# A hybrid S5 / RG-LRU decoder layer: the feed-forward block's first operands placed over other memory, and the S5 stages set later

## The chip, the cores and the metric

The kernel runs on one core of one Trainium2 chip. The metric is the device time of one execution in microseconds (us); every number here is in us unless it says otherwise. The engines are named as in the profile: PE (TensorE, matrix multiply), PEld (its weight loads), DVE (VectorE), ACT (ScalarE), POOL (GpSimd), SP (SyncE, which issues every DMA here; SPq is its queue).

## The reference

One layer on x of 2048 tokens by 1024 channels, float32:

```python
h = rms_norm(x, norm1_g)
proj = h @ w_in                      # 1024 -> 1536: u | xr | yr, 512 each
s5_out  = s5_mixer(u, ...)           # 32 groups of 16 channels, 64 complex states each,
                                     # a linear scan over time, then GELU and a sigmoid GLU
lru_out = rglru_mixer(xr, yr, ...)   # causal conv(4), sigmoid gates, gated linear scan, times GELU(yr)
mix = concat(rms_norm(s5_out), rms_norm(lru_out))
x = x + mix @ w_out
h2 = rms_norm(x, norm2_g)
x = x + (silu(h2 @ w_gate) * (h2 @ w_up)) @ w_down     # 1024 -> 2816 -> 1024
return rms_norm(x, final_g)
```

## The kernel before

**Precision and tiles.** Every large product is made of three matmuls on a high and a low part: high weight by high operand, high by low, low by high. ACT casts the high part (`whi`, `xh`), DVE or POOL subtracts it from the source to get the low part (`wlo`, `xl`). One matmul is 128x128 by 128x512. The 2048 tokens are four blocks of 512.

**Stages.** (1) Input projection, block by block (`in_tb`, 12 units of 24 matmuls each), with the recurrence's convolution, gates, decay and scan. Beside it `s5_build`, `s5_table`, `s5_w`, `s5_cp`, `s5_k`, `s5_i` and `s5_d_build` make S5's matrices and store them in the DRAM tensor `md`. (2) S5 in two halves (g = 0: blocks 0 and 1; g = 1: blocks 2 and 3), eight steps each: `s5_in` (matmuls and products), `s5_scan` (scans on DVE, products on DVE and POOL), `s5_out` (line 864 multiplies by `s_s`). The input goes through the DRAM tensor `ub`, the output through `zb`; `zload` (line 897) reads `zb` back. (3) `glu_tb` makes S5's GLU of a block and the mix: `norm_split` writes the normed operands of w_out, for even blocks in eight pieces of pool Q (`aH`, `aL`), for odd ones in `actH` and `actL` of pool A. (4) `out_pair(0)` for blocks 0 and 1 and `out_pair(2)` for 2 and 3: eight units m for each block; the evacuation (line 992) adds x, line 994 stores the sum in `x1d`, and `SumSq.finish` stores the row of scales in `r2d` (line 272). (5) The feed-forward block (FFN): gate and up products as Strassen-like products 1 to 7 on 2x2 blocks, in the order `PRODS = (1, 6, 2, 7, 5, 4, 3)`, for p = 0 (blocks 0 and 1), then p = 1; each of 11 steps s has a gate unit and an up unit of 84 matmuls (line 1209). (6) w_down (line 1349) and the final norm.

**FFN's first operands.** `combos` loads two rows of x1d and the scales into `hx` (line 1078, 1080), DVE norms them (line 1084), and DVE and POOL make the sums of the blocks in tiles `ht` (lines 1092 to 1095). For p = 0 `x_first` does so for k = 0 to 3 and splits the results at once into `xh` and `xl` (`split_x2`, lines 1049 and 1050), except products 5 and 3 (`LATE`), which go to the DRAM tensor `xcd` (line 1116), since their tiles lie in pool D2, over pool A; `x_load` reads these back (line 1139) and splits them. For p = 1 `x_ahead` stores all seven products early in FFN, and `x_load` reads them when p = 0 is done.

**What sets the order.** Every piece of work is put on a list with a time, `at(t, fn)`, in plan units. The list is run in the order of time, and a scheduler that models the engines then orders each engine's instructions; so the times are priorities. `ts0 = 130` is the time of the first S5 half, `tb_(t) = 18 + 2.2 * t` that of the pieces of the build. Each engine and SP's queue then run strictly in their order.

**Memory.** Pools are opened as a stack from the left (P, Q, L) and from the right (A, W, then S). `open_d1` closes L, Q and S and opens D1 over them, with the tiles of FFN; a tile of D1 waits for the readers of what lay there.

Of the kernel before, what the change touches and what calls it, by code (L numbers as in the profile page):

```python
# [9 lines left out]
F32 = mybir.dt.float32  # L10
# [7 lines left out]
SEQ, DM, TB = 2048, 1024, 512  # L18
# [41 lines left out]
class Plan:  # L60
# [3 lines left out]
    def at(self, t, fn):  # L64
        self.ev.append((t, len(self.ev), fn))
# [10 lines left out]
PRODS = (1, 6, 2, 7, 5, 4, 3)  # L76
# [3 lines left out]
def build(tc, nc, I, O, ctx):  # L80
# [10 lines left out]
    sA, sQ = ExitStack(), ExitStack()  # L91
    A = sA.enter_context(tc.tile_pool(name="A", bufs=1, side="right", reuse_waits="tile"))
    Q = sQ.enter_context(tc.tile_pool(name="Q", bufs=1, reuse_waits="tile"))
# [1 line left out]
    actL = A.tile([128, 8, TB], F32, name="actL")  # L95


    def piece(i, j, name):
        return Q.tile([128, 2, TB], F32, tag=f"pc{i}{j}", name=f"{name}{j}")

    pieces = {}

    def area(i):
        def chunk(k):
            if (i, k // 2) not in pieces:
                pieces[i, k // 2] = piece(i, k // 2, "aH" if i == 0 else "aL")
            return pieces[i, k // 2][:, k % 2, :]
        return chunk
# [100 lines left out]
    def mm3(ps, u, ks, H, L, first, last):  # L209
        n = len(ks)  # L210
        for i, (kw, kx) in enumerate(ks):
            part = u.parts[kw // 4]
            for j, (w, x) in enumerate((("hi", H), ("hi", L), ("lo", H))):
                PE.matmul(ps, lhsT=part[w][:, kw % 4, :], rhs=r_(x(kx)),  # L214
                          start=first and i == 0 and j == 0, stop=last and i == n - 1 and j == 2)
# [73 lines left out]
    def load_chunk(src, b, k, pool=A, tag="xc", bufs=4):  # L289
        t = pool.tile([128, TB], F32, tag=tag, name=tag, bufs=bufs)  # L290
        SP.dma_start(t, src[k * 128:(k + 1) * 128, b * TB:(b + 1) * TB])
        return t
# [261 lines left out]
        TS(out=cL, in0=s, scalar1=8.0, scalar2=None, op0=ALU.mult)  # L554
        TS(out=cLh, in0=s, scalar1=-4.0, scalar2=None, op0=ALU.mult)

    ts0 = 130

    def s5_start():
        with tc.issue_after(last["rs"]):  # L560
            s5_build()

    def tb_(t):
        return 18 + 2.2 * t

    at(18, s5_start)
    at(12.0, lru_decay)
    for half in range(2):
        for lev in range(7):
            at(tb_(1.0 + 5 * half + 0.7 * lev), lambda half=half, lev=lev: s5_table(half, lev))  # L570
# [27 lines left out]

    at(1.0, lru_start)
    xrp = [piece(0, i, "xr") for i in range(2)]  # L600
    v_xr = [t.rearrange("p a b -> p (a b)")[:, 0:TB + 4] for t in xrp]
    v_xh = [piece(1, 2, "xh"), piece(0, 2, "xh")]
    v_y, v_us = piece(0, 3, "y"), piece(1, 1, "us")
    v_hh, v_hl = piece(1, 0, "hh"), piece(1, 3, "hl")
# [281 lines left out]
    def pair(b):  # L886
        return (areaH, areaL) if b % 2 == 0 else (chunks_of(actH), chunks_of(actL))
# [76 lines left out]
    def out_bank():  # L964
        n = last["bank"] = last.get("bank", -1) + 1
        return acc() if n % 4 < 2 else aux("gt", 2)

    def out_pair(b0, t0):

        sums = {b: SumSq(8, ("sum", "sumh")[b % 2], dv=b >= NB - 2) for b in (b0, b0 + 1)}
        blocks = (b0, b0 + 1)
        order = [(m, b) for b in blocks for m in (0, 1)]
        order += [(m, b) for m in range(2, 6 if b0 == 0 else 8) for b in blocks]
        if b0 == 0:
            order += [(m, b) for b in blocks for m in (6, 7)]
        units = {}
        for n, (m, b) in enumerate(order):  # L980
            cur = C[b]
            t = t0 + n * 8 * PT + (32 * PT if b0 == 0 and n >= 12 else 0)
            if m not in units:
                units[m] = Unit(t, I["w_out"][m], 8, GP if m % 3 == 1 else DV)

            def prod(m=m, b=b, cur=cur, u=units[m]):
                cur["o", m] = out_bank()
                mm3(cur["o", m], u, [(k, k) for k in range(8)], *pair(b), True, True)

            def post(m=m, b=b, cur=cur):  # L990
                xc = cur.pop(("x", m))
                DV.tensor_tensor(out=xc, in0=cur.pop(("o", m)), in1=xc, op=ALU.add)
                sums[b].add(xc)
                SP.dma_start(x1d[b // 2][128 * m:128 * m + 128, TB * (b % 2):TB * (b % 2) + TB], xc)

            at(t - 5, lambda m=m, b=b, cur=cur: cur.__setitem__(("x", m), load_chunk(xT, b, m)))
            at(t, prod)
            at(t + 8 * PT + 0.5, post)
            if m == 7:
                at(t + 8 * PT + 4.0, lambda b=b: sums[b].finish(r2d[b // 2][TB * (b % 2):TB * (b % 2) + TB]))  # L1000
# [20 lines left out]
    D = {}  # L1021

    def open_d1():
        sL.close()
        sQ.close()
        sS.close()
        D["1"] = sD1.enter_context(tc.tile_pool(name="D1", bufs=1, reuse_waits="tile"))

# [4 lines left out]
    def d1(tag, bufs=1, dt=F32, w=TB):  # L1033
        return D["1"].tile([128, w], dt, tag=tag, name=tag, bufs=bufs)
# [3 lines left out]

    def xtile(c, j, k, dt=R, name=None):

        tag = f"x{c}{j}{k}"
        return D["2" if j in LATE else "1"].tile([128, TB], dt, tag=tag, name=name or tag, bufs=1)

    BANK = {1: "A", 2: "A", 6: "B", 7: "B", 4: "B", 5: "C", 3: "C"}
    FIRST = (1, 6, 5)
    LATE = (5, 3)

    def split_w(raw, eng, hi, lo):
        AC.copy(hi, raw)  # L1049
        eng.tensor_tensor(out=lo, in0=raw, in1=hi.bitcast(F32), op=ALU.subtract)  # L1050
        return hi, lo
# [19 lines left out]
    def combos(p, k, t):  # L1071

        cur = {}

        def load():
            for i in range(2):
                cur[i] = d1("hx", 3, w=2 * TB)
                SP.dma_start(cur[i], x1d[p][128 * (k + 4 * i):128 * (k + 4 * i) + 128])
            rs = cur["rs"] = d1("hx", 3, w=2 * TB)
            SP.dma_start(rs, r2d[p].unsqueeze(0).to_broadcast([128, 2 * TB]))  # L1080

        def norm():
            for i in range(2):
                DV.scalar_tensor_tensor(out=cur[i], in0=cur[i], scalar=pc("g2", k + 4 * i), in1=cur["rs"],
                                        op0=ALU.mult, op1=ALU.mult)

        def sums():
            a, c = cur[0], cur[1]
            b11, b12, b21, b22 = a[:, 0:TB], a[:, TB:], c[:, 0:TB], c[:, TB:]
            T = {j: d1("ht", 4) for j in (5, 7, 6, 4)}  # L1090
            a, c = (GP.tensor_tensor, (GP if p else DV).tensor_tensor)
            a(out=T[5], in0=b12, in1=b11, op=ALU.subtract)
            c(out=T[7], in0=b22, in1=b12, op=ALU.subtract)
            c(out=T[6], in0=T[7], in1=b11, op=ALU.add)
            a(out=T[4], in0=b21, in1=T[6], op=ALU.subtract)
            T.update({1: b11, 2: b21, 3: b22})
            cur["T"] = T

        at(t - 5.0, load)
        at(t, norm)  # L1100
        at(t + 0.5, sums)
        return cur

    def split_x2(p, j, k, src, eng):
        H, L = (xtile(c, j, k) for c in "hl")
        X[p, j, k] = split_w(src, eng, H, L)

    def x_first(p, t):
        for k in range(4):
            tk = t + 6.0 * k  # L1110
            cur = combos(p, k, tk)

            def fin(k=k, cur=cur):
                for i, j in enumerate(PRODS):
                    if j in LATE:
                        SP.dma_start(xcd[p, k, :, j - 1, :], cur["T"][j])
                    else:
                        split_x2(p, j, k, cur["T"][j], GP if i % 3 == 2 else DV)

            at(tk + 2.0, fin)  # L1120

    def x_ahead(p, ts):
        for k in range(4):
            cur = combos(p, k, ts[k])

            def fin(k=k, cur=cur):
                for j in PRODS:
                    SP.dma_start(xcd[p, k, :, j - 1, :], cur["T"][j])

            at(ts[k] + 4.0, fin)  # L1130

    def x_load(p, times):
        for i, j in enumerate(times):
            for k in range(4):
                cur = {}

                def load(j=j, k=k, cur=cur):
                    cur["t"] = d1("ht", 4)
                    SP.dma_start(cur["t"], xcd[p, k, :, j - 1, :])

                t = times[j] + (k - 4) * 0.65
                at(t - 5.0, load)
                at(t - 1.5, lambda i=i, j=j, k=k, cur=cur: split_x2(p, j, k, cur["t"], GP if (i + k) % 2 else DV))
# [121 lines left out]
    def down(t0):  # L1265
# [93 lines left out]
        def row_tile(p, q, i):  # L1359
            r = RR[p, q, i] = xtile("hl"[p], {2: 7, 0: 5, 1: 4, 3: 3}[q], i, F32, f"r{q}")  # L1360
            return r
# [86 lines left out]
    gt = {}  # L1448
# [6 lines left out]
    tD = T  # L1455

    at(tC - 128 * PT + 4.0, open_d1)
    at(tC + 1.0, open_d2)
    x_first(0, tC - 128 * PT + 12.0)
    x_load(0, {j: gt[0, 0, 0, j] for j in LATE})  # L1460
    x_ahead(1, [gt[0, 3 + 2 * k, 0, 1] for k in range(4)])
    x_load(1, {j: gt[1, 0, 0, j] for j in PRODS})
    for p in range(2):
# [5 lines left out]
    pl.run()  # L1469
    sD2.close()  # L1470
    sD1.close()


def layout(x, norm1_g, w_in, s5_lambda_re, s5_lambda_im, s5_log_step, s5_b_re, s5_b_im, s5_c_re, s5_c_im,
# [78 lines left out]
```

## Time and profile before

| what | us |
|---|---|
| time, median of 3 runs | 2196.97 (2190.81 to 2200.07) |
| the profiled execution's own time | 2196.63 |
| its span, first to last instruction | 2194.9 |
| PE busy | 1964.2 (89% of the span) |
| DVE busy | 1207.0 (55%) |
| POOL busy | 1016.9 (46%) |
| ACT busy | 802.2 (37%) |
| last matmul of w_out for blocks 2 and 3 | 768 |
| first FFN matmul | 771 |

Busy times are summed over instructions; matmuls overlap in PE's pipeline, so a busy PE is not a PE at its peak, and the granted clock (PEclk) says how fast it ran. "DVE x <- PE y" in the views of waits reads: idle time of DVE ahead of x that ended when PE finished y.

### The profile page before, as it was taken

Reading aid. Unit: us, or ns where it says so; the run is one execution under the profiler, and the core shown is the slowest. Engines: PE = TensorE matmul, PEld = TensorE weight load, DVE = VectorE, ACT = ScalarE, POOL = GpSimd, SP = SyncE. Lnnn points to the kernel's source line nnn. Section 1 sums busy time; section 2 is a strip of 40 time slices with the busy share of each in tenths; the row PEclk is TensorE's granted clock in tenths of the full one; section 3 lists DMA queues with packets and bytes.
Section 4 is the critical chain, followed back from the end, with each engine's and each line's share of the span. In section 5 each row is a group of like instructions: output and inputs, shape, how many; then the busy total and the mean of one; then the engine's idle time right before and its main releaser. Section 6 shows DMA issues by size and latency. Waiting matters only on the chain.

```text
span 2194.9 us, 25988 instructions
## 1 busy us (share of the span) xinstructions
PE 1964.2 (89%) x8600; PEld 1564.3 (71%) x8600; DVE 1207.0 (55%) x1927; ACT 802.2 (37%) x1308; POOL 1016.9 (46%) x836
## 2 busy tenths in 40 slices
PE   5749898987989938799999999999999999999996
PEld 4637676765767816577777777777777788888785
DVE  5997676388447377444444474444444535654644
ACT  4535553463253123232232252232232343333331
POOL 1576255389533067654554561322312436644442
PEclk8969998988999958899999999999999999999998
DMA  8646997976543458644444484444444568854733
GB/s 290 215 151 202 297 253 260 223 193 189 148 122 117 158 187 282 220 163 145 144 158 144 156 260 131 137 142 133 144 131 130 171 221 317 298 171 143 238 101 101
DMA packets 259814, 405.21 MB, mean 185 GB/s; under 512 B 60224, under 2 KB 82016, under 8 KB 259680
## 3 DMA queue, kind: packets, MB, share of 16 engines
q1 hardware_dynamic: 259680, 403.56, 58.2%
q8 instruction: 67, 1.10, 0.2%
q14 instruction: 67, 0.55, 0.1%
HBM read 280.51 MB, written 122.96 MB: 184 GB/s over the span
## 4 chain that ended last, share of the span: by engine, by line
PE 67%; DVE 13%; DMA 7%; POOL 5%; ACT 3%; issue 3%; SPq 1%; POOLq 0%; DVEq 0%; ACTq 0%
PE acc L1209 9%; PE gt L1209 9%; PE y L1209 9%; PE acc L214 8%; PE v L1209 5%; PE nm L1209 5%; PE acc L1349 4%; PE y L1349 4%; PE gt L1349 4%; PE gt L214 3%; PE nm L1349 2%; PE v L1349 2%; POOL s_s L854 1%; DMA ht<-xcd 1%; DMA wraw<-w_in 1%
## 5 line engine op out<-in xcount | busy, mean ns | idle before, releaser
L1222 POOL TENSOR_TENSOR t<-t 128x512 f32<-128x512 f32 x66 | 100.8, 1528 | 348.6 <-DVE t L1248 219.4
L1049 ACT CAST whi<-ws 128x512 fp32r<-128x512 f32 x176 | 109.3, 621 | 347.3 <-PE y L1209 89.5
L214 PE MATMUL acc<-actH,whi 128*128 128x512 f32 x424 | 177.8, 421 | 43.1 <-DVE gy L712 14.8
L214 PE MATMUL acc<-actL,whi 128*128 128x512 f32 x424 | 177.3, 418 | 17.8 <-DVE actL L296 16.5
L214 PE MATMUL acc<-actH,wlo 128*128 128x512 f32 x424 | 174.9, 413 | 2.3 <-DMA wlo<-wlc 2.0
L1050 DVE TENSOR_TENSOR wlo<-ht,whi 128x512 fp32r<-128x512 f32 x112 | 106.8, 955 | 125.9 <-ACT whi L1049 123.8
L1049 ACT CAST whi<-ht 128x512 fp32r<-128x512 f32 x154 | 95.0, 618 | 167.8 <-PE nm L1349 72.4
L1209 PE MATMUL y<-xh,whi 128*128 128x512 f32 x308 | 125.5, 407 | 30.6 <-ACT xh L1049 16.3
L1050 DVE TENSOR_TENSOR wlo<-ws,whi 128x512 fp32r<-128x512 f32 x176 | 133.2, 757 | 33.0 <-ACT whi L1049 32.8
L1050 DVE TENSOR_TENSOR wlo<-wraw,whi 128x512 fp32r<-128x512 f32 x88 | 71.3, 810 | 143.4 <-ACT whi L1049 143.3
L1209 PE MATMUL acc<-xh,wlo 128*128 128x512 f32 x308 | 123.8, 402 | 10.3 <-DVE wlo L1050 10.3
L214 PEld LDWEIGHTS acc<-actH,whi 128*128 128x128 f32 x424 | 85.0, 201 | 67.3 <-issue 24.1
L1050 POOL TENSOR_TENSOR wlo<-ht,whi 128x512 fp32r<-128x512 f32 x42 | 58.3, 1389 | 159.2 <-ACT whi L1049 159.1
L1209 PE MATMUL acc<-xh,whi 128*128 128x512 f32 x308 | 124.1, 403 | 8.2 <-ACT xh L1049 6.6
L1209 PE MATMUL y<-xl,whi 128*128 128x512 f32 x308 | 124.1, 403 | 7.1 <-DVE xl L1050 7.1
L1209 PE MATMUL acc<-xl,whi 128*128 128x512 f32 x308 | 123.7, 402 | 7.0 <-DVE xl L1050 7.0
L1209 PE MATMUL y<-xh,wlo 128*128 128x512 f32 x308 | 123.7, 402 | 2.6 <-DVE wlo L1050 2.6
L1209 PE MATMUL gt<-xh,whi 128*128 128x512 f32 x308 | 121.4, 394 | 0.0
L1209 PE MATMUL gt<-xh,wlo 128*128 128x512 f32 x308 | 121.3, 394 | 0.0
L1209 PE MATMUL gt<-xl,whi 128*128 128x512 f32 x308 | 121.3, 394 | 0.0
L214 PEld LDWEIGHTS acc<-actL,whi 128*128 128x128 f32 x424 | 85.3, 201 | 40.6 <-DVE actL L296 22.7
L1049 ACT CAST whi<-wraw 128x512 fp32r<-128x512 f32 x88 | 54.6, 621 | 159.6 <-PE y L1209 53.0
(459 smaller groups left out, 5432.4 us busy)
## 6 DMA issues: line engine op xcount, KB each, us to landing
td<-t SPq DMA_DIRECT2D x154, 256.0 KB, 2.1
ht<-td SPq DMA_DIRECT2D x154, 256.0 KB, 3.2
wraw<-w_down SPq DMA_DIRECT2D x99, 256.0 KB, 4.8
wraw<-w_in SPq DMA_DIRECT2D x96, 256.0 KB, 4.8
scd<-ws SPq DMA_DIRECT2D x88, 256.0 KB, 2.1
ws<-scd SPq DMA_DIRECT2D x88, 256.0 KB, 2.7
wlo<-wlc SPq DMA_DIRECT2D x72, 256.0 KB, 5.3
xc<-xT SPq DMA_DIRECT2D x56, 256.0 KB, 4.7
```

Source lines behind the costliest of these rows:

```text
L214: PE.matmul(ps, lhsT=part[w][:, kw % 4, :], rhs=r_(x(kx)), start=first and i == 0 and j == 0, stop=last and i == n - 1 and j == 2)
L854: GP.tensor_tensor(out=sv[64 * ri:64 * ri + 64, gl, :, 1:], in0=a[p], in1=c[p], op=op)
L1049: AC.copy(hi, raw)
L1050: eng.tensor_tensor(out=lo, in0=raw, in1=hi.bitcast(F32), op=ALU.subtract)
L1209: PE.matmul(ps, lhsT=a[:, k, :], rhs=x, start=j in FIRST and k == 0 and i == 0, stop=k == 3 and i == 2, skip_group_check=True)
L1222: (DV if q == 0 else GP).tensor_tensor(out=g, in0=c, in1=g, op=ALU.mult)
L1349: PE.matmul(BK[p][i], lhsT=a[:, i, :], rhs=x, start=j in FIRST and s == 0 and v == 0, stop=s == NSL - 1 and v == 2, skip_group_check=True)
```

## The change

Four things are edited. The tiles of products 7 and 4 (`INQ`) for FFN's operands take the eight pieces of pool Q, two k in each, and Q stays open to the end, so that D1 lies over L and S only. `x_first` splits products 1, 6 and 2 (`AHEAD`) at once and sends 7, 5, 4 and 3 through `xcd`, where before only 5 and 3 went. `out_pair(2)` takes units 6 and 7 block by block, as `out_pair(0)` did. And the build's stretch grows from 2.2 to 2.9 plan units a step, with the first S5 half at 150 instead of 130.

```diff
@@ -95,8 +95,8 @@
     actL = A.tile([128, 8, TB], F32, name="actL")
 
 
-    def piece(i, j, name):
-        return Q.tile([128, 2, TB], F32, tag=f"pc{i}{j}", name=f"{name}{j}")
+    def piece(i, j, name, dt=F32):
+        return Q.tile([128, 2, TB], dt, tag=f"pc{i}{j}", name=f"{name}{j}")
 
     pieces = {}
 
@@ -554,14 +554,14 @@
         TS(out=cL, in0=s, scalar1=8.0, scalar2=None, op0=ALU.mult)
         TS(out=cLh, in0=s, scalar1=-4.0, scalar2=None, op0=ALU.mult)
 
-    ts0 = 130
+    ts0 = 150
 
     def s5_start():
         with tc.issue_after(last["rs"]):
             s5_build()
 
     def tb_(t):
-        return 18 + 2.2 * t
+        return 18 + 2.9 * t
 
     at(18, s5_start)
     at(12.0, lru_decay)
@@ -973,9 +973,8 @@
         sums = {b: SumSq(8, ("sum", "sumh")[b % 2], dv=b >= NB - 2) for b in (b0, b0 + 1)}
         blocks = (b0, b0 + 1)
         order = [(m, b) for b in blocks for m in (0, 1)]
-        order += [(m, b) for m in range(2, 6 if b0 == 0 else 8) for b in blocks]
-        if b0 == 0:
-            order += [(m, b) for b in blocks for m in (6, 7)]
+        order += [(m, b) for m in range(2, 6) for b in blocks]
+        order += [(m, b) for b in blocks for m in (6, 7)]
         units = {}
         for n, (m, b) in enumerate(order):
             cur = C[b]
@@ -1022,7 +1021,6 @@
 
     def open_d1():
         sL.close()
-        sQ.close()
         sS.close()
         D["1"] = sD1.enter_context(tc.tile_pool(name="D1", bufs=1, reuse_waits="tile"))
 
@@ -1038,12 +1036,20 @@
 
     def xtile(c, j, k, dt=R, name=None):
 
+        if j in INQ:
+
+            key = c, j, k // 2
+            if k % 2 == 0:
+                D[key] = piece("hl".index(c), 2 * INQ.index(j) + k // 2, name or f"x{c}{j}", dt)
+            return D[key][:, k % 2, :]
         tag = f"x{c}{j}{k}"
         return D["2" if j in LATE else "1"].tile([128, TB], dt, tag=tag, name=name or tag, bufs=1)
 
     BANK = {1: "A", 2: "A", 6: "B", 7: "B", 4: "B", 5: "C", 3: "C"}
     FIRST = (1, 6, 5)
     LATE = (5, 3)
+    INQ = (7, 4)
+    AHEAD = (1, 6, 2)
 
     def split_w(raw, eng, hi, lo):
         AC.copy(hi, raw)
@@ -1112,7 +1118,7 @@
 
             def fin(k=k, cur=cur):
                 for i, j in enumerate(PRODS):
-                    if j in LATE:
+                    if j not in AHEAD:
                         SP.dma_start(xcd[p, k, :, j - 1, :], cur["T"][j])
                     else:
                         split_x2(p, j, k, cur["T"][j], GP if i % 3 == 2 else DV)
@@ -1457,7 +1463,7 @@
     at(tC - 128 * PT + 4.0, open_d1)
     at(tC + 1.0, open_d2)
     x_first(0, tC - 128 * PT + 12.0)
-    x_load(0, {j: gt[0, 0, 0, j] for j in LATE})
+    x_load(0, {j: gt[0, 0, 0, j] for j in PRODS if j not in AHEAD})
     x_ahead(1, [gt[0, 3 + 2 * k, 0, 1] for k in range(4)])
     x_load(1, {j: gt[1, 0, 0, j] for j in PRODS})
     for p in range(2):
@@ -1469,6 +1475,7 @@
     pl.run()
     sD2.close()
     sD1.close()
+    sQ.close()
 
 
 def layout(x, norm1_g, w_in, s5_lambda_re, s5_lambda_im, s5_log_step, s5_b_re, s5_b_im, s5_c_re, s5_c_im,
```

In what the scheduler makes of it, line numbers past 1040 are 6 higher than before, those from 976 to 1020 one lower. DVE, at the end of w_out for blocks 2 and 3 (xc: an evacuation; sum, sumh: sums of squares; hx: the norm of a round; ht: its sums; xl: a low part). Before:

```order
L992 TENSOR_TENSOR xc<-gt,xc 128x512
L255 TENSOR_TENSOR sum<-sum,sq 128x512
L992 TENSOR_TENSOR xc<-gt,xc 128x512
L1084 SCALAR_TENSOR_TENSOR hx<-hx,par 128x1024 x2
L227 TENSOR_SCALAR nm<-nm 128x4
L255 TENSOR_TENSOR sumh<-sumh,sq 128x512
L1050 TENSOR_TENSOR xl_5838<-hx,xh_5837 128x512
L1093 TENSOR_TENSOR ht<-hx 128x512
```

and now:

```order
L991 TENSOR_TENSOR xc<-acc,xc 128x512
L1090 SCALAR_TENSOR_TENSOR hx<-hx,par 128x1024 x2
L255 TENSOR_TENSOR sum<-sum,sq 128x512
L1056 TENSOR_TENSOR wlo<-wraw,whi 128x512
L1056 TENSOR_TENSOR xl_6076<-hx,xh_6075 128x512
L1099 TENSOR_TENSOR ht<-hx 128x512
L991 TENSOR_TENSOR xc<-gt,xc 128x512
L1056 TENSOR_TENSOR wlo<-ws,whi 128x512
L1100 TENSOR_TENSOR ht<-ht,hx 128x512
```

Before, this is the norm of k = 0, behind the last evacuation. Now it is that of k = 3, with two evacuations still to come; the norms of k = 0, 1 and 2 stand 8, 6 and 3 evacuations ahead of that one.

SP's queue, the loads of products from xcd (ht<-xcd) where FFN begins. Before:

```order
L1078 DMA hx<-x1d_85 128x1024 x2
L1139 DMA ht<-xcd 128x512 x2
L1080 DMA hx<-r2d_87 128x1024
L1139 DMA ht<-xcd 128x512
L1167 DMA scd<-ws 128x512
L1139 DMA ht<-xcd 128x512 x3
```

and now:

```order
L993 DMA x1d_85<-xc 128x512
L1084 DMA hx<-x1d_85 128x1024
L1145 DMA ht<-xcd 128x512
L1173 DMA scd<-ws 128x512
L1145 DMA ht<-xcd 128x512
L1163 DMA wraw<-w_gate 128x512
L1122 DMA xcd<-ht 128x512
L1145 DMA ht<-xcd 128x512
L993 DMA x1d_85<-xc 128x512
L1173 DMA scd<-ws 128x512
L1145 DMA ht<-xcd 128x512
```

The loads, 8 before and 16 now, begin behind the last but one store of x1d (unit 7 of block 3 is the last), where before they came after all of w_out and of the four rounds.

POOL, at the last low part of the mix of blocks 0 and 1 (actL; s_k, s_s, s_wr and s_wi are S5's second half). Before:

```order
L854 TENSOR_TENSOR s_s<-s_tb,s_wi 64x2x128 x2
L854 TENSOR_TENSOR s_s<-s_ta,s_wr 64x2x128 x2
L303 TENSOR_TENSOR actL<-nf,actH 128x512
L812 TENSOR_TENSOR s_wr<-s_wr,s_ta 128x256
L813 TENSOR_TENSOR s_wi<-s_wi,s_tb 128x256
L854 TENSOR_TENSOR s_s<-s_tb,s_wi 64x2x128 x2
```

and now:

```order
L303 TENSOR_TENSOR actL<-nf,actH 128x512
L812 TENSOR_TENSOR s_wr<-s_wr,s_ta 128x256
L813 TENSOR_TENSOR s_wi<-s_wi,s_tb 128x256
L832 COPY s_s<-cy 64x2 x4
L833 TENSOR_TENSOR s_k<-cy,mi 128x2
```

Before, one S5 step ended behind it, now three do. In the two orders the first 372 instructions of DVE are the same, and on PE all from FFN's 104th matmul to the end.

## The prediction

> **What bounds the kernel now.** I read the page's slices first, then busy time by stage, then what TensorE (PE) waits for in the worst stage. Section 2 of the page, 40 slices of 55 us, tenths busy, and the granted clock:
>
> ```profile
> PE   5749898987989938799999999999999999999996
> PEclk8969998988999958899999999999999999999998
> ```
>
> From slice 16 on PE is full at full clock; the bad places are the first four slices, slices 9 and 10, and slices 14 and 15 (760 to 880 us), where the feed-forward (FFN) begins. There I cut the time where the output projection ends (768.0), where FFN's first full runs begin (836.9), and where the loss ends (908.1), counting FFN's matmuls alone (columns: stretch, length, PE busy (count), weight loads, clock, DMA share, GB/s):
>
> ```profile
> 768.00:836.90 68.90, 21.57 (x43) 11.00 (x43) 0.58 0.63 209
> 836.90:908.10 71.20, 55.12 (x210) 43.09 (x211) 0.86 0.82 276
> 908.10:988.60 80.50, 78.48 (x337) 62.86 (x336) 1.00 0.48 161
> ```
>
> The third row is the steady state: 80.5 / 337 = 0.2389 us a matmul. So the first stretch is worth 43 x 0.2389 = 10.3 us and loses 58.6; the second is worth 50.2 and loses 21.0. Together 79.6 us, the largest loss in the trace outside the first 250 us. What PE waits for from 768 to 910:
>
> ```profile
> PE y L1209 <- ACT xh L1049: 16.3, 4, 5.1
> PE acc L1209 <- DVE wlo L1050: 10.3, 1, 10.3
> PE y L1209 <- DVE xl L1050: 7.1, 4, 3.3
> PE acc L1209 <- DVE xl L1050: 7.0, 3, 5.3
> ```
>
> xh and xl are FFN's first operands, high and low part. They are made in four rounds (k = 0 to 3), which follow one another on VectorE (DVE) at the pace of their first instruction, the norm of line 1084; the queue says when they could have begun and what the first load waited for (last row: total, times, longest):
>
> ```profile
> 792.20 2.48 DVE L1084 SCALAR_TENSOR_TENSOR hx<-hx,par 128x1024 f32<-128x1024 f32 x2
> 805.17 2.48 DVE L1084 SCALAR_TENSOR_TENSOR hx<-hx,par 128x1024 f32<-128x1024 f32 x2 [4.05 <-DMA hx<-r2d]
> 818.50 2.48 DVE L1084 SCALAR_TENSOR_TENSOR hx<-hx,par 128x1024 f32<-128x1024 f32 x2 [4.42 <-DMA hx<-r2d]
> 709.53 0.27 SPq L272 DMA_DIRECT2D r2d<-row  x1
> SPq L1078 <- PE gt L214: 2.7, 2, 2.4
> 690.87 0.74 DVE L301 SCALAR_TENSOR_TENSOR nf<-wg,par,rs 128x512 f32<-128x512 f32 x1
> 746.02 11.06 PE acc L214 x48
> ```
>
> A round takes 13.2 us. Its inputs, x1d and r2d of blocks 0 and 1, are complete once the store of 709.53 has landed, 58.5 us before 768. The first load waited for PE's read of block 2's operands: FFN's memory lies over them. The last two rows serve below: the last norm of block 3's mix on DVE, and two units (48 matmuls) of the output projection, 5.53 us each.
>
> **The change, part by part.**
>
> *First operands out of the pieces' memory.* The D1 pool now lies over the L and S pools alone, which the last mix of block 3 leaves at 691 us, and in the new order of instructions the four norms stand among the evacuations of the second output projection (w_out) instead of behind them. Is there time? Rounds at 13.2 us from 709.5 plus the median landing of hx (row below) give norms at 715, 728, 742 and 755; the order puts the fourth behind the evacuation of the third unit from the end, 10 us before 768. Its splits take a round's 8.1 us of DVE (worked out below). So the operands of products 1, 6 and 2 are ready when PE wants them. Is there room? The stage before, all engines (PE, weight loads, DVE, ACT, POOL, clock, DMA), and the moved groups as they ran from 768 to 836.9 (busy us, mean ns | idle before):
>
> ```profile
> hx<-r2d SPq DMA_DIRECT2D x8, 512.0 KB, 5.8
> 712.00:768.00 56.00, 56.00 (x245) 45.55 (x244) 17.50 (x25) 11.30 (x18) 4.03 (x4) 1.00 0.49 155
> L1084 DVE SCALAR_TENSOR_TENSOR hx<-hx,par 128x1024 f32<-128x1024 f32 x10 | 12.5, 1294 | 10.7 <-DMA hx<-r2d 10.7
> L1050 DVE TENSOR_TENSOR xl<-hx,xh 128x512 fp32r<-128x512 f32 x4 | 7.0, 1740 | 0.0
> L1093 DVE TENSOR_TENSOR ht<-hx 128x512 f32<-128x512 f32 x4 | 7.1, 1763 | 0.0
> L1094 DVE TENSOR_TENSOR ht<-ht,hx 128x512 f32<-128x512 f32 x4 | 3.7, 928 | 0.3
> L1050 DVE TENSOR_TENSOR xl<-ht,xh 128x512 fp32r<-128x512 f32 x9 | 10.1, 1123 | 2.3 <-ACT xh L1049 2.2
> L1092 POOL TENSOR_TENSOR ht<-hx 128x512 f32<-128x512 f32 x4 | 8.8, 2210 | 15.1 <-DVE hx L1084 15.1
> L1166 POOL TENSOR_TENSOR ws<-wraw 128x512 f32<-128x512 f32 x2 | 3.0, 1516 | 1.2 <-DVE nv L235 1.2
> L1095 POOL TENSOR_TENSOR ht<-hx,ht 128x512 f32<-128x512 f32 x4 | 6.5, 1623 | 4.5 <-DVE ht L1094 4.5
> ```
>
> DVE gets four rounds of 2 x 1.294 + 1.740 + 1.763 + 0.928 + 1.123 = 8.1 us, 32.6 in all, beside its 17.5 of 56: it fits. POOL gets some 22 us and eight weight sums of 1.5 beside its 4. What waits behind a norm that waits for its hx is an evacuation, and PE has four banks, so it can run three units, 16.6 us, before it misses one. I let the end of w_out slip by 1 us (0 to 13).
>
> *Products 7, 5, 4 and 3 through memory.* Before, only 5 and 3 of these went out to xcd and back. Now all four do: 16 tiles, 8 stores and 8 loads more, through four ht buffers, each load behind the split of the one four earlier. The nearest row is the same loading at the change from p = 0 to 1 (first and last row of 24 loads):
>
> ```profile
> 1267.71 2.02 SPq L1139 DMA_DIRECT2D ht<-xcd  x3
> 1303.17 1.57 SPq L1139 DMA_DIRECT2D ht<-xcd  x2
> ht<-xcd SPq DMA_DIRECT2D x36, 256.0 KB, 3.5
> ```
>
> 24 tiles in 37 us is 1.54 us a tile, 24.7 for 16. The loads stand in SP's queue around the last two stores of x1d, so the first goes out 1 us before PE ends w_out, and the last tile is split 24.7 + 3.5 + 2 us later, at +29. Ahead of it PE has the 72 other matmuls of the unit and up to 30 that the order draws forward from the up unit, about 24 us. So 5 us of waiting, and 2 more because the sums of blocks 2 and 3 stand in PE's queue there behind a chain of small DVE instructions. I take 7, with 0 (the loads keep ahead) and 24 (a full cadence that hides nothing) as ends. This replaces the 58.6: **-51.6**.
>
> *The second stretch, 21.0 us.* DVE's norms for p = 1 stand in front of FFN's own splits and wait for their loads; they stand in nearly the same rows as before, and from there to the end PE's order is unchanged. I keep 21 (12 to 32).
>
> *Pieces kept open, and the new order of units 6 and 7.* Tiles of 7 and 4 take block 2's pieces. With (6, 7) of block 2 ahead of (6, 7) of block 3, PE leaves those two units, 11 us, before w_out's end, ahead of the first load of product 7. Cost nothing; the cover is those 11 us. Weights 6 and 7 then need four high parts at once, which is all there are, so FFN's first weight is cast as unit 6 of block 3 ends, 5 us before it is needed.
>
> *Build of S5 over a longer stretch, S5 later.* Up to 216 us (the first row below is the last instruction of the common part) DVE, which bounds there (105.16 busy of 110 us), has the same instructions in the same order. So the costliest stretch of the start gains nothing. Behind it the second half of the matrices and the first S5 half move back by 20 to 35 matmuls, and some of the second half's S5 steps leave the mix stage:
>
> ```profile
> 216.19 1.23 DVE L696 SCALAR_TENSOR_TENSOR r<-r,T 128x1024 f32<-128x1024 f32 x1 [4.15 <-ACT r L150]
> 95.00:205.00 110.00, 69.79 (x274) 52.39 (x273) 105.16 (x155) 46.90 (x69) 81.03 (x76) 0.77 0.54 171
> PE y L864 <- POOL s_s L854: 5.7, 3, 2.6
> PE v L803 <- DMA mi<-md: 3.9, 1, 3.9
> PE y L864 <- DMA mo<-md: 3.8, 1, 3.8
> L864 PE MATMUL y<-s_s,mo x36: 270/275/582, 502.4 to 559.6; 128*128 128x128 f32 x36
> 502.00:566.00 64.00, 44.73 (x251) 34.62 (x249) 54.96 (x112) 18.47 (x37) 56.39 (x79) 0.89 0.60 168
> ```
>
> The waits are PE's from 250 to 475 us: S5 costs it 13.4 there. Moved loads meet less traffic, but scans of block 3 more S5: I take -3 (-13 to +10). From 502 to 566 POOL is busy 56.39 of 64 with S5 steps and the mix's low parts. Seven and a bit of eight steps stood ahead of the last mix operand; now five do. But the steps also start later, by about one step. A step has 8 of these matmuls, and 36 of them took 57 us: 12.7 us a step. I take -2 (-24, two steps off, to +13, one step late), since the remaining steps must still end before zb is read back.
>
> Sum: -51.6 + 1 + 0 - 3 - 2 = -55.6, against the profiled execution's 2196.63 (span 2194.9 and 1.7 around it; the median of the runs shown, 2196.97, is 0.3 above): **2141 us**.
>
> **The rivals.**
> *The load cadence bounds FFN's start.* If nothing hides behind the 16 tiles, 24 instead of 7: 2158. For it: one queue, four buffers, and DMA share already 0.82 in the second stretch. Against: PE finds 100 matmuls there that need no late tile.
> *DVE and POOL get in each other's way in w_out.* Rows of the same instructions alone:
>
> ```profile
> 742.04 0.69 DVE L255 TENSOR_TENSOR sum<-sum,sq 128x512 f32<-128x512 f32 x1 [0.76 <-ACT sq L253]
> 743.87 1.29 POOL L189 TENSOR_TENSOR wlo<-wraw,whi 128x512 fp32r<-128x512 f32 x1 [29.18 <-ACT whi L188]
> ```
>
> Beside POOL's work a subtraction took 1.74, not 0.69. If the two are served one at a time, the stage's need is DVE 4 x (2.6 + 4 x 0.69) = 21.4 and its own 17.5, POOL 12 x 1.29 and 8 x 1.29 = 25.8 and its own 4: 68.7 us in 56, so w_out's end slips by 13: 2153. It decides from the point where an evacuation comes three units late. The Trainium skill (SBUF — State Buffer, Who interferes with whom) says just this: a VectorE instruction with two SBUF inputs and a GpSimd one that reads SBUF exclude each other for the whole instruction. The 1.74 agrees; by that rule the time would be 2153. Against it, 17.5 counts evacuations from PSUM, and the rounds may run late by a few us unseen.
> *S5 out of the way gains in full.* 13 and 24 instead of 3 and 2: 2109.
> *The operands come no earlier.* If a reader of L or S memory, or the x1d stores ahead in SP's queue, hold the first hx load to the end of w_out, the 58.6 stays: about 2192, the same.
> *Slower: S5's output late.* The zb stores of the first half's second part now stand in SP's queue right ahead of the loads of z for blocks 0 and 1, with weights behind both. Every us that S5's last step is late stops all loads. It would have to cost more than 55 + 11 us to end slower; the last S5 output moves by 28 matmuls, 6.5 us at full rate, so this takes a stall ten times that.
>
> **How the numbers follow.** 0.5% is 11 us, about what a measurement of this kernel tells from no change. Forecast (2125 to 2150): 0.55. Cadence 0.13, DVE and POOL 0.12, S5 in full 0.12, no earlier 0.05, slower 0.03. Faster is all but the last two: 0.92. The range takes the ends of the start (7 to 24) and of w_out (13) upwards, 2170, and S5's gains downwards, 2109; beyond it lie some 0.15.
>
> **What would show it.** Right: norms of k = 0 to 3 before w_out's last matmul; FFN's first 43 matmuls in some 17 us; clock 0.9 or more in that stretch; the stretch behind it still losing about 20; w_out's 245 matmuls in 56 to 58 us; identical times up to 216 us. Wrong: hx loads that wait for PE; PE waiting for xl of product 5 or 3 for more than 15 us; w_out with PE idle; z loads late and the output projection's first unit past 505 us.

## The result, and the profile after

The changed kernel takes 2144.72 us (median, 2140.97 to 2145.59) against 2198.52 of the kernel before, timed beside it: a ratio of 0.9759, 95% interval 0.9732 to 0.9785. The forecast was 2141. Its profiled execution took 2144.24 us, span 2142.5, 52.4 less than the span before. The slices of the page after:

```profile
PE   6849999887989987999999989999999999999996
PEclk8968999988999989999999999999999999999998
```

Counted from 0, slices 14 to 16 held 3, 8 and 7 at a clock of 5, 8 and 8 tenths before; now they hold 8, 7 and 9 at 8, 9 and 9. FFN's start is shorter, and something is still lost in slices 14 and 15 (750 to 857 us). Line numbers above 1040 are 6 higher than before, so FFN's matmuls are line 1215. Its start, cut behind the 43rd, the 168th and the 252nd matmul, and 80.5 us behind that (columns: stretch, length, PE busy (count), weight loads, clock, DMA share, GB/s):

```profile
769.80:790.70 20.90, 12.35 (x43) 9.57 (x43) 0.76 0.88 286
790.70:822.50 31.80, 29.89 (x127) 23.21 (x125) 1.00 0.75 249
822.50:853.70 31.20, 21.83 (x86) 16.67 (x85) 0.89 0.87 307
853.70:934.20 80.50, 78.48 (x337) 62.78 (x336) 1.00 0.61 206
```

The steady row is the same as before, 337 in 80.5 us. By it the first 43 matmuls are worth 10.3 us and lose 10.6 (58.6 before); the next 125 lose 1.9 and the next 84 lose 11.1, together 13.0 (21.0 before). What PE waits for from 690 to 870 us:

```profile
PE acc L1215 <- DVE wlo L1056: 7.4, 2, 7.1
PE nm L269 <- DVE nv L236: 5.9, 1, 5.9
PE acc L214 <- POOL wlo L189: 4.3, 1, 4.3
PE acc L214 <- ACT whi L188: 2.0, 1, 2.0
```

No row names xh or xl: the first operands no longer hold PE. The second row lies in FFN's first 43 matmuls, and the 7.1 of the first row behind its 168th. The last two rows are new, and lie in the output projection w_out. Its last 96 matmuls (two units of two blocks, behind the 2016th matmul of line 214) before and after:

```profile
745.90:768.10 22.20, 22.20 (x97) 17.76 (x95) 1.00 0.56 177
```

```profile
737.70:769.90 32.20, 25.29 (x97) 19.20 (x95) 0.89 0.85 280
```

So w_out's end slips by 10.0 us. These 96 matmuls begin 8.2 us earlier than before, which is put down to S5's part here. The account: -48.0 (first stretch), +10.0 (w_out), -8.0 (second stretch), -8.2 (S5) = -54.2; from there on 1.8 is given back, at the change to p = 1 and behind, which leaves the 52.4.

### The profile page after: what moved, and what is told of

It is laid out like the page before. It is cut to its first block, busy times and chain, and to the rows that moved or that the text cites. A ratio compares the mean times of both kernels' runs of the same rounds, so it can differ in the third digit from the quotient of the medians.

```text
span 2142.5 us, 26006 instructions
## 1 busy us (share of the span) xinstructions
PE 1949.6 (91%) x8600; PEld 1556.4 (73%) x8600; DVE 1220.4 (57%) x1927; ACT 797.4 (37%) x1308; POOL 1012.7 (47%) x836
## 4 chain that ended last, share of the span: by engine, by line
PE 63%; DVE 14%; DMA 10%; issue 4%; POOL 3%; ACT 3%; SPq 2%; POOLq 0%; DVEq 0%; ACTq 0%
PE acc L1215 9%; PE y L1215 9%; PE gt L1215 9%; PE acc L214 5%; PE v L1215 5%; PE nm L1215 5%; PE y L1355 4%; PE acc L1355 4%; PE gt L1355 4%; PE nm L1355 2%; PE v L1355 2%; PE gt L214 2%; DMA wraw<-w_in 1%; DMA wlo<-wlc 1%; DMA hx<-r2d 1%
## 5 line engine op out<-in xcount | busy, mean ns | idle before, releaser
L214 PE MATMUL acc<-actH,whi 128*128 128x512 f32 x416 | 172.9, 418 | 36.7 <-DVE gy L712 14.1
L214 PE MATMUL acc<-actL,whi 128*128 128x512 f32 x416 | 172.8, 416 | 22.4 <-DVE actL L296 19.6
L214 PE MATMUL acc<-actH,wlo 128*128 128x512 f32 x416 | 170.6, 411 | 1.3 <-DMA wlo<-wlc 1.1
L1056 DVE TENSOR_TENSOR wlo<-wraw,whi 128x512 fp32r<-128x512 f32 x88 | 75.8, 861 | 138.6 <-ACT whi L1055 138.5
```

The lines of the kernel that those rows point to most:

```text
L214: PE.matmul(ps, lhsT=part[w][:, kw % 4, :], rhs=r_(x(kx)), start=first and i == 0 and j == 0, stop=last and i == n - 1 and j == 2)
```

## Experiments: which part does what

Four kernels were timed together with the kernel before (median 2192.65 us in these runs). The us that a kernel takes off are worked out from its ratio here and below, and kernels that were timed in different sets are compared by their ratios.

**FFN's part alone.** The changed kernel, with

```diff
-    ts0 = 150
+    ts0 = 130
...
-        return 18 + 2.9 * t
+        return 18 + 2.2 * t
```

> The FFN part of the change alone (operands over L and S, products 7, 5, 4, 3 through memory, the new order of units 6 and 7), with the old places of S5 and of its build (ts0 130, 2.2 per step). Theory A, the parts add: in the trace of after the FFN start loses 24 us instead of 80, and w_out runs 10 us late in its last three units, both by themselves. Then this kernel saves 56 - 10 = 46 of the 53 us: ratio 0.979, about 2152 us, and its first 490 us are those of before. Rival B, the slip of w_out comes only because the S5 part made the stages before it earlier: then this kernel saves all 56, ratio 0.975, 2143 us, and S5's part is worth nothing at the end.

Measured: 2152.09 us, ratio 0.9824 (0.98 to 0.9848), 38.6 us off. Rival B falls: the last 96 matmuls of w_out take 32.2 us here too (742.5 to 774.7), so the slip belongs to FFN's part. They begin 3.4 us earlier than before, though PE's order up to there is that of before: single traces scatter by as much. Theory A's figure of 46 is above the interval's end of 44.

**S5's part alone.** The kernel before, with the two numbers of the change.

> The S5 part alone (ts0 150, 2.9 per step) in the kernel before. Theory A: the input projection ends 17 us earlier as in after, 9 of it is given back in the mix, GLU and the first output projection, and 8 are left at the end: ratio 0.996, about 2190 us. Rival B, what is given back comes from the FFN part: then 17 us are left, ratio 0.992, 2181 us. Rival C, the projection's gain is made up before the FFN begins because VectorE is behind there anyway: 2198 us, the same.

Measured: 2170.72 us, ratio 0.9901 (0.9882 to 0.992), 21.7 us off. All three theories' figures are too small. In its trace the first matmul of line 214 behind the input projection (the 1153rd) starts 21.6 us earlier than before, w_out ends 13.8 earlier, and the kernel 25.4 earlier. So 7.8 is given back on the way without FFN's part (rival B's reason is wrong; part of it is work put behind that matmul, see the next run), and another 12 is gained where FFN begins: the profiled execution before has there a wait of 10.3 us for a weight's low part (shown in the prediction), and this one no wait above 3.2 in the same stretch. That is one trace of each kernel, and why S5's place changes this wait is not shown.

**S5 later, the build packed.** The changed kernel with 2.2 instead of 2.9 plan units a step, ts0 kept at 150.

> After, with the build of S5's matrices packed again as before (2.2 instead of 2.9 per step), the first S5 half still later (ts0 150). Theory A: the gain of 17 us in the input projection comes from the later S5 half, and the spread of the build does nothing by itself, so the time is that of after, ratio to before 0.976. Rival B: the gain comes from the spread, because VectorE, POOL and ScalarE bound the stretch from 216 us on; then this kernel loses it, ratio 0.980 to 0.983, 2153 to 2160 us.

Measured: 2140.73 us, ratio 0.9767 (0.9746 to 0.9787). Theory A: the gain is that of the later first half, and the spread of the build shows nothing. The stretch from 216 us, where the order of after begins to differ (this kernel's does so at 288), to the 1680th matmul of line 214, within one matmul, in four kernels, in this order: before, after, this one, FFN's part alone (all engines: PE, weight loads, DVE, ACT, POOL, clock, DMA share, GB/s):

```profile
216.00:658.10 442.10, 386.40 (x1898) 306.55 (x1898) 270.56 (x502) 209.25 (x323) 239.31 (x282) 0.93 0.74 211
```

```profile
216.00:650.20 434.20, 380.52 (x1901) 300.58 (x1900) 277.54 (x502) 207.05 (x323) 230.26 (x282) 0.94 0.76 214
```

```profile
216.00:645.40 429.40, 380.37 (x1902) 305.05 (x1901) 275.89 (x502) 209.30 (x324) 236.31 (x282) 0.93 0.76 217
```

```profile
216.00:655.00 439.00, 383.21 (x1901) 305.06 (x1900) 269.61 (x502) 209.04 (x323) 239.36 (x282) 0.94 0.75 212
```

The same matmuls take 427.6 to 434.2 us in the four kernels with ts0 = 150 (S5's part alone 428.3, the next kernel 427.6), and 439.0 and 442.1 with ts0 = 130. The four differ by up to 7 us though three of them have one order there, and the two by 3, so any two of these traces give a gain between 5 and 14 us. More traces narrow it. Ten of the kernels of this document, after among them, run PE's matmuls of that stretch in one order. From the start of the 594th matmul of all (at 213 us), the last that this order shares with the old one, to the start of the 1680th of line 214 they take 430.5 to 436.7 us, 432.9 in the mean; the two kernels with the old order take 444.9 and 441.4. So S5's part gains about 10 us there. The cut is made late because the 1153rd matmul of line 214 has 542 other matmuls ahead of it in the new order and 592 in the old: the 17.1 us by which after is early there is in part work put behind it.

**FFN's operands over Q again.** The changed kernel with its memory undone, and only products 1, 6 and 2 made ahead:

```diff
-    INQ = (7, 4)
+    INQ = ()
...
 def open_d1():
         sL.close()
+        sQ.close()
         sS.close()
```

> After, with the place of FFN's first operands undone: the D1 pool lies over the Q pool (block 2's operands) again, as in before, while products 7, 5, 4 and 3 still go through memory and only 1, 6 and 2 are made ahead. Theory A, the memory is what lets the norms stand among w_out's evacuations: undone, the first norm waits for PE's last read of block 2's operands again, and the first stretch loses 45 to 59 us again; with the S5 part's 8 us the time is 2183 to 2198 us, ratio 0.993 to 1.0. Rival B, the shorter list of products made ahead (three instead of five) is most of the gain: then FFN's start loses some 25 us as in after, and the time is 2145 to 2155 us.

Measured: 2177.31 us, ratio 0.9932 (0.9914 to 0.995): the lower edge of theory A's ratios, and far from rival B. FFN's first 43 matmuls take 65.5 us as before (65.9), and w_out's last 96 take 23.2:

```profile
754.40:819.90 65.50, 21.60 (x44) 10.97 (x44) 0.58 0.69 237
```

The place in memory is the cause of the 48 us and, with them, of w_out's slip; a shorter list of products made ahead gains nothing by itself.

## Experiments: what is left at FFN's start

The next four were timed together too (before: 2191.53 us).

**Five products made ahead**, so that 8 tiles go through memory instead of 16.

```diff
-    AHEAD = (1, 6, 2)
+    AHEAD = (1, 6, 2, 7, 4)
```

> After, with five products made ahead as in before (1, 6, 2, 7, 4), so that only 5 and 3 go out through memory, in the new place. It undoes the part of the change that sends 7 and 4 through memory. Theory A: the 16 tiles through memory cost FFN's start next to nothing (PE in after waits there for no xl tile at all), while two more products of splits on VectorE and POOL among w_out's last units push w_out's end out further: some 3 to 6 us slower than after, 2148 to 2151 us, ratio 0.977 to 0.980. Rival B: the cadence of the loads from memory bounds FFN's start; then with 8 tiles instead of 16 it is 5 to 12 us faster than after, 2133 to 2140 us.

Measured: 2141.14 us, ratio 0.9765 (0.9748 to 0.9782), that of after: neither theory's time. The first 43 matmuls take 29.3 us (760.7 to 790.0) instead of 20.9, with a wait of 6.8 for a high part xh, and w_out's last 96 take 28.5 instead of 32.2. The last round's norm now comes behind w_out's end (at 771.75 us, 11 behind it), which fits both. So this run moves two things, and halving the loads is not tested alone. That their cadence does not bound FFN's start in after rests on the trace of after, where no row of PE's waits names a tile that they bring.

**Units 6 and 7 in turn**, as before:

```diff
-        order += [(m, b) for m in range(2, 6) for b in blocks]
-        order += [(m, b) for b in blocks for m in (6, 7)]
+        order += [(m, b) for m in range(2, 6 if b0 == 0 else 8) for b in blocks]
...
```

> After, with the order of units 6 and 7 in the second output projection as in before (block 2 and block 3 in turn). Theory A: the order of these two units does nothing by itself (the stretch is held by weight parts and norms): within 4 us of after, ratio 0.974 to 0.978. Rival B: PE waits 4.3 us for the low part of unit 7's weight because the new order wants it 5.5 us earlier; then undoing it takes away that wait and the slip of w_out, -5 to -9 us, ratio 0.972 or less. Rival C: block 2's pieces are left 5.5 us later, and the loads into them hold SP's queue: +5 us.

Measured: 2144.1 us, ratio 0.978 (0.9763 to 0.9796). Rival B's wait shrinks from 4.3 to 1.8 us, w_out's last 96 matmuls take 24.3 us, but nothing is won: the first 252 of FFN take 96.1 us instead of 83.9. PE finds a late DVE a stage further on: it waits 8.1 us for a sum of squares (line 255) and 7.0 and 3.8 us for an evacuation of FFN.

**Unit 7's low part on DVE instead of POOL:**

```diff
-                units[m] = Unit(t, I["w_out"][m], 8, GP if m % 3 == 1 else DV)
+                units[m] = Unit(t, I["w_out"][m], 8, GP if m % 3 == 1 and m < 7 else DV)
```

> After, with the low part of weight 7 of the output projections made on VectorE instead of POOL. Theory A: w_out's slip (PE's 4.3 us for POOL's low part of unit 7) comes from POOL's queue, where the products of the first operands stand ahead; then this takes 4 us off, 2140 us, ratio 0.974. Rival B: the high part on ScalarE, which is cast late behind the xh parts (PE waits 2.0 us for it just before), and the norm that waits for hx on VectorE set the end; then the low part is as late on VectorE, behind the norm's wait: same time as after, within 2 us, and PE waits 4 us or more for wlo of VectorE in that place.

Measured: 2140.35 us, ratio 0.9761 (0.9744 to 0.9778), that of after, and PE's wait in that place only changes its name:

```profile
PE acc L214 <- DVE wlo L189: 4.3, 2, 4.1
```

Rival B. What comes ahead of that weight shows in the trace of after, on SP, DVE, ACT and POOL in turn (start, duration, what it waited for; the first row is the longest wait of SP's queue from 731 to 738 us):

```profile
SPq L1163 <- DVE wlo L189: 3.4, 1, 3.4
737.78 0.47 SPq L1086 DMA_DIRECT2D hx<-r2d  x1
744.52 2.48 DVE L1090 SCALAR_TENSOR_TENSOR hx<-hx,par 128x1024 f32<-128x1024 f32 x2 [4.78 <-DMA hx<-r2d]
745.84 0.62 ACT L1055 CAST xh<-hx 128x512 fp32r<-128x512 f32 x1 [6.31 <-DVE hx L1090]
747.56 0.61 ACT L188 CAST whi<-wraw 128x512 fp32r<-128x512 f32 x1
745.89 2.24 POOL L1098 TENSOR_TENSOR ht<-hx 128x512 f32<-128x512 f32 x1 [3.75 <-DVE hx L1090]
751.48 1.71 POOL L189 TENSOR_TENSOR wlo<-wraw,whi 128x512 fp32r<-128x512 f32 x1
```

SP stands ahead of the copy of r2d, waiting for DVE to be done with a weight's low part, and the third round's norm waits for that copy. Behind the norm on ACT stands the cast of unit 7's weight, and on POOL, behind three slow instructions of the round and of a weight sum, its low part. In this trace a norm that waits on one engine holds w_out's weights on two others.

**Norms for p = 1 behind evacuations.** They are the rounds of `x_ahead`. Each is ordered behind the last evacuation of an FFN step:

```diff
-            cur = combos(p, k, ts[k])
+            cur = combos(p, k, ts[k], ("ev", 2 + 2 * k))
...
+            if after is not None:
+                with tc.issue_after(last[after]):
+                    norms()
```

> After, with VectorE's norms for p = 1 ordered behind the last evacuations of FFN's steps 2, 4, 6 and 8 instead of among the first steps. Theory A: the second loss of FFN's start (11 us between its 168th and 252nd matmul) is the norms' wait for their loads at the head of VectorE's queue, with the low parts of FFN's weights queued behind; then it goes: 8 to 11 us faster than after, 2134 to 2137 us, ratio 0.971 to 0.972, and the 252 matmuls lose 13 us instead of 24. Rival B: what VectorE or the weights' own loads are short of there is throughput or DMA; then the loss stays, moved by a few us at most, and the time is that of after.

Measured: 2128.99 us, ratio 0.9714 (0.9694 to 0.9735), 10 us off after's: theory A. In after, two rows of DVE, and FFN's third stretch in this kernel (its line 1222), beside the 31.20 us shown above:

```profile
822.38 2.48 DVE L1090 SCALAR_TENSOR_TENSOR hx<-hx,par 128x1024 f32<-128x1024 f32 x2 [3.27 <-DMA hx<-r2d]
840.98 4.26 DVE L1090 SCALAR_TENSOR_TENSOR hx<-hx,par 128x1024 f32<-128x1024 f32 x2 [5.79 <-issue]
```

```profile
815.50:836.20 20.70, 19.69 (x85) 15.67 (x84) 1.00 0.51 170
```

The 84 matmuls now run at the steady pace, 20.7 for 20.1 us. The clock, 0.89 in that stretch, is 1.00, and PE's wait of 7.1 us for a low part is gone.

## Experiments: the waits taken away

The last four (before: 2194.12 us).

**r2d's row loaded once.** `combos` loaded the same row over 128 partitions anew in each round.

```diff
-                cur[i] = d1("hx", 3, w=2 * TB)
+                cur[i] = d1("hx", 2, w=2 * TB)
...
-            rs = cur["rs"] = d1("hx", 3, w=2 * TB)
-            SP.dma_start(rs, r2d[p].unsqueeze(0).to_broadcast([128, 2 * TB]))
+            if k == 0:
+                X["rs", p] = d1("rs", 1, w=2 * TB)
+                SP.dma_start(X["rs", p], r2d[p].unsqueeze(0).to_broadcast([128, 2 * TB]))
+            cur["rs"] = X["rs", p]
```

> After, with r2d's row loaded over all partitions once for p = 0 and once for p = 1 into a buffer of its own, instead of anew in each of the four rounds (hx keeps two buffers and rs gets the third: the same memory, six loads of 512 KB less). Theory A: the norms of rounds 2 and 3 hang on the load hx<-r2d, which SP issues behind the residual loads (xc<-xT, themselves behind the stores of x1d); the x1d loads have landed 5 to 10 us before. Then the norm at 744.5 comes 5 us or more earlier, the weights of unit 7 with it, and w_out's slip of 7 us shrinks to 2 to 4; the norms for p = 1 wait less too. Together 5 to 10 us faster than after, ratio 0.972 to 0.974. Rival B: the slip is VectorE's and POOL's work (4 rounds beside each other at 1.8 us instead of 0.7), not a wait: then the norms come a little earlier, w_out ends as late as in after, ratio 0.976. Rival C: with two hx buffers the next x1d loads wait for the round before, and the norms are as late as now: 0.976 to 0.978.

Measured: 2133.25 us, ratio 0.9713 (0.9696 to 0.9729), 10 us off after's. The size is theory A's, the place only in part. The third round's norms now stand at 733.33 and 736.75, against 744.52; PE's wait for POOL's low part halves to 2.2 us, but w_out's last 96 matmuls still take 30.1 us. The casts of w_out's weights on ACT now stand behind another part of the third round, the cast of a sum that waits for DVE:

```profile
742.66 0.62 ACT L1055 CAST xh<-ht 128x512 fp32r<-128x512 f32 x1 [3.99 <-DVE ht L1102]
743.86 1.12 ACT L188 CAST whi<-wraw 128x512 fp32r<-128x512 f32 x2
```

The rest is FFN's start, 76.5 us for 252 matmuls instead of 83.9: PE's wait of 5.9 us for the sums' chain (line 269) shrinks to 0.5.

**Both: late norms, one row.**

> The norms for p = 1 ordered late and r2d's row loaded once, together. If the two take away different waits (the second loss of FFN's start; w_out's slip), their gains add: 10 us for the first as measured, 3 to 6 for the second: ratio 0.968 to 0.970, about 2122 us. If the row loaded once only helped the norms for p = 1, nothing is added to the late norms: 0.971.

Measured: 2119.95 us, ratio 0.9664 (0.9645 to 0.9682). They add, and more than forecast: 21 us off after's, where each alone gave 10. FFN's first 252 matmuls take 64.1 us, 3.9 more than at the steady pace; w_out's last 96 still take 30.4.

**The four rounds for p = 0 wholly on DVE:**

```diff
-            a, c = (GP.tensor_tensor, (GP if p else DV).tensor_tensor)
+            a = c = (GP if p else DV).tensor_tensor
...
-                        split_x2(p, j, k, cur["T"][j], GP if i % 3 == 2 else DV)
+                        split_x2(p, j, k, cur["T"][j], DV)
```

> After, with the four rounds for p = 0 wholly on VectorE (the sums of products 5 and 4 and the splits of product 2 move there from POOL: 12 instructions). Theory A, VectorE and POOL exclude each other in two-input instructions: a round on VectorE then takes 2.6 + 7 x 0.69 = 7.4 us, as little as the 8.1 it takes now with fewer instructions, because POOL's part of the rounds no longer stretches them to 1.8 us each; VectorE's share of w_out does not grow and the time is that of after or up to 4 us better, ratio 0.974 to 0.976; the subtractions of L1056 and L1099 last about 0.7 us where no other POOL work lies beside them. Rival B, the two run side by side and the 1.8 us have another cause: the instructions stay at 1.2 to 1.8, a round becomes 2.6 + 7 x 1.4 = 12.4 us, 17 us more VectorE work in the stage: w_out slips 5 to 12 us more, ratio 0.978 to 0.981.

Measured: 2133.44 us, ratio 0.9723 (0.9707 to 0.974), 8 us off after's, twice theory A's best (the two intervals overlap a little, so the trace has to carry it); rival B falls. From 700 to 782 us, after and this kernel, and one group of it with the same instruction in after (PE, weight loads, DVE, ACT, POOL; then clock, DMA share, GB/s):

```profile
700.00:782.00 82.00, 69.83 (x295) 55.06 (x293) 62.99 (x72) 24.01 (x42) 40.93 (x25) 0.94 0.81 267
L1056 DVE TENSOR_TENSOR xl<-hx,xh 128x512 fp32r<-128x512 f32 x4 | 6.0, 1499 | 0.0
```

```profile
700.00:782.00 82.00, 73.36 (x309) 58.43 (x309) 62.71 (x100) 29.17 (x51) 24.25 (x16) 0.92 0.86 289
L1056 DVE TENSOR_TENSOR xl<-hx,xh 128x512 fp32r<-128x512 f32 x8 | 7.1, 882 | 0.0
```

DVE runs 100 instructions in the time of 72 (13 of the 28 more are small ones of the sums' chain, near 0.16 us each), the mean of these subtractions falls from 1.50 to 0.88 us, and POOL has 16.7 us less to do. In this kernel w_out's last 96 matmuls take 23.3 us: nearly all of the slip is gone, though the norms still wait for r2d.

```profile
732.80:756.10 23.30, 22.65 (x97) 17.64 (x95) 1.00 0.85 287
726.81 0.32 SPq L1086 DMA_DIRECT2D hx<-r2d  x1
733.99 2.48 DVE L1090 SCALAR_TENSOR_TENSOR hx<-hx,par 128x1024 f32<-128x1024 f32 x2 [3.63 <-DMA hx<-r2d]
```

The last two rows are the third round's copy and norm. The copy goes out 6.0 us ahead of w_out's last 96 matmuls, where in after it went out 0.1 behind their start, and the norm comes 1.2 us behind that start instead of 6.9. Two things differ ahead of the copy: SP no longer waits 3.4 us for DVE, and the copy stands ahead of a residual load (xc<-xT) behind which it stood in after. So without POOL's share of the rounds 8.9 of the slip's 10.0 us go, and without the repeated copies of r2d alone 2.1. How much of the 8.9 is due to the shorter instructions, and how much to the new order of SP's and POOL's queues, no run tells apart. FFN's first 252 matmuls still take 86.4 us, since its two waits are untouched.

**All three.**

> All three together: norms for p = 1 late, r2d's row once, rounds for p = 0 wholly on VectorE. Where each takes away a wait of its own: 14 to 18 us faster than after, ratio 0.967 to 0.969. If work on VectorE holds FFN's start (rival B of the rounds on VectorE), it ends behind the version without that move by 5 us or more.

Measured: 2116.08 us (2111.62 to 2116.89), ratio 0.964 (0.9625 to 0.9655), 26 us off after's, more than the 14 to 18 expected, and the fastest of all; against the kernel without the rounds on DVE (0.9664) it gains 5, at intervals that overlap. w_out's last 96 take 23.2 us, and FFN's start 66.4 for 60.2 of work:

```profile
752.60:819.00 66.40, 61.12 (x253) 48.22 (x253) 0.97 0.61 204
```

## Why the prediction was right, and where not

- *First operands out of the pieces' memory.* Right in the mechanism: the norms came at 708, 723, 745 and 761 us for a forecast of 715, 728, 742 and 755, all before w_out's last matmul, and with the memory undone the loss is back. Of 58.6 us, 10.6 stayed (forecast 7, of 0 to 24), and the clock of that stretch was 0.76 where 0.9 or more was forecast.
- *The loads ahead of PE, 5 of the 7.* Wrong in its cause, though near in size. No wait for a late tile shows in after, so the rival of the cadence falls. The only waits in this stretch are that of the other 2, the sums' chain, at 5.9 us, and one of 0.3; another 2.1 is PE's busy time, 12.35 us for work of 10.3.
- *w_out's end, 1 (0 to 13).* Mis-sized: 10.0. The stretch forecast at 56 to 58 us took 66.1 (703.8 to 769.9), and PE idled there, which the prediction had named as a sign of being wrong. The step that failed is the sentence "What waits behind a norm that waits for its hx is an evacuation, and PE has four banks". A weight part was also behind it, on ACT and POOL, and has no bank to cover it. The rival that DVE and POOL get in each other's way had a slip of 13 as its price. It came nearer for this term: without POOL's share of the rounds 8.9 of the 10.0 go, though that run also changes the order of the queues. The Trainium skill (SBUF — State Buffer, Who interferes with whom) says that a two-input VectorE instruction and a GpSimd one that reads SBUF exclude each other. The traces agree in direction: the mean of 1.50 us fell to 0.88 as POOL's part left, and single subtractions alone take 0.68.
- *Second stretch kept at 21 (12 to 32).* Measured 13.0, within its ends. The cause named, norms for p = 1 ahead of FFN's splits, is shown: the 11.1 us behind the 168th matmul go when the norms go late.
- *S5, -3 and -2.* The step that failed is the price of the moved first half: after's trace gives -8.2 where -5 was forecast, twelve traces give about 10 for it, and S5's part alone takes 21.7 off the time, some of it at FFN's start. The prediction priced the waits of PE for S5's tiles (13.4 us); these do not explain the gain. From 216 us to the cut shown above the waits ahead of lines 803 and 864 sum to 19.2 us before and 8.3 in after, but to 25.2 in the kernel with the build packed, and that one gained 12.7 all the same, 6.0 of it as shorter matmul time (386.40 to 380.37 us for 1898 and 1902) and the rest as idle time. Why is open.
- *Same times up to 216 us* held within 3 us: the 480th matmul of line 214 starts at 219.6 before and 216.9 after.
- *A reading.* "From slice 16 on PE is full at full clock" is one slice early: the page before has 7 tenths at a clock of 8 in slice 16. No term of the sum rests on it.

The sum came out 3.2 us low against the span, since the slip (+9.0 against its term) and the first stretch (+3.6) were set off by the second stretch (-8.0) and S5 (-3.2); 1.8 came behind. That the total came so near is in part luck: the agreement is better than its terms are. That the two parts' gains (38.6 and 21.7) sum to more than the 53 of the whole fits with part of S5's gain lying at FFN's start, where FFN's part leaves less to win; no run tests this by itself.

## What to carry to other kernels

Memory that a later stage takes over decides when that stage's preparation can start; before changing what is prepared, look whom the first load waits for. When preparation moves beside another stage, follow everything behind its first wait on every engine in order, weight parts as well as evacuations, and load once what several rounds share. Between DVE and POOL it can pay to leave an instruction on the busier one, if the other would stretch it: the run here that did so gained 8 us, its new order of the queues included.

## What was not expected of the hardware

Moving 12 two-input instructions from POOL to DVE cost DVE no time in the same 82 us (62.99 us for 72 instructions, 62.71 for 100; leaving out the small ones, 59 and 74). What the window held on DVE beside them, after and with the rounds on DVE:

```profile
L189 DVE TENSOR_TENSOR wlo<-wraw,whi 128x512 fp32r<-128x512 f32 x4 | 3.8, 951 | 0.0
L991 DVE TENSOR_TENSOR xc<-gt,xc 128x512 f32<-128x512 f32 x6 | 4.1, 681 | 0.0
```

```profile
L189 DVE TENSOR_TENSOR wlo<-wraw,whi 128x512 fp32r<-128x512 f32 x4 | 2.7, 678 | 0.0
L991 DVE TENSOR_TENSOR xc<-gt,xc 128x512 f32<-128x512 f32 x6 | 4.1, 679 | 0.0
```

The weights' low parts, both of whose inputs lie in SBUF, go from 0.95 to 0.68 us; the evacuations, with one input from PSUM, last 0.68 in both.
